# Fifty-six scratch stores of an NSA + RWKV-7 hybrid block move from SyncE's queue to ScalarE's

## The chip, the cores and the metric

One core of one Trainium2 chip. The metric is the device time in microseconds (us) of one execution of the whole program; lower is better. TensorE is called PE here, VectorE DVE, ScalarE ACT, GpSimd POOL, and SyncE, which in this kernel does nothing but issue transfers, SP.

## The reference

One transformer layer on 1024 tokens of width 1024. Two token mixers read the same normed input: native sparse attention (8 query heads, 2 key-value heads; a compressed, a selected and a sliding-window branch, each weighted by a sigmoid gate) and an RWKV-7 recurrence (8 heads of 64). Their outputs are projected, gated by sigmoids, summed, and projected back; a convolutional feed-forward network of width 2816 follows.

```python
h = _rms_norm(x, norm_mix[l])
u = h @ w_in[l]
q, kc, vc, ks, vs, kw, vw, nsa_gl, rw, merge = _split(u, IN_SPLITS)
o_nsa = _nsa(q, kc, vc, ks, vs, kw, vw, nsa_gl, qk_gain[l], cmp_pe[l], cmp_w1[l], cmp_w2[l])
o_rwkv, v_first = _rwkv7(rw, v_first, vres, rwkv_mu[l], ...)
gates = jax.nn.sigmoid(merge.astype(jnp.float32)).astype(x.dtype).reshape(B, S, 2, D)
y = gates[:, :, 0] * (o_nsa @ proj_nsa[l]) + gates[:, :, 1] * (o_rwkv @ proj_rwkv[l])
x = x + y @ w_out[l]
x = x + _conv_ffn(_rms_norm(x, norm_ffn[l]), ffn_up[l], ffn_conv[l], ffn_down[l])
```

With 16 blocks of 64 keys and a top-k of 16 every causal block is selected, so the selected branch is causal attention over all keys.

## The kernel before

Everything is kept transposed: features on the 128 partitions, tokens along the free axis, in two halves of 512 tokens (`H[0]`, `H[1]`; the index `h` in the code). Matrices are split into a 16-bit high and low part, so that one product is three matmuls of 128x512 (`mm3`, line 279, or `mm3s`, line 299, for several products side by side). `wload` loads a 128x1024 weight tile (`wraw`), ACT makes the high part `whi` (line 267), DVE the low part `wlo` (line 269).

The stages, in the order of time:

- Norm of the input and the first projections; then `attention()` (from about 150 to 610 us). For each of four head pairs it takes maxima of scores (`mp`, lines 602 to 609), then makes exp tiles `ph` and `pf` on ACT (lines 672, 673), `pl` on DVE (674), and multiplies with the values (677 to 682). At the end of a pair, four transposes per half go through ACT into `oT`, a tile with one buffer, and from there to scratch memory `onsa_d` (lines 701 to 704).
- Woven between the pieces of attention are "fillers": projections of the RWKV input (`zproj`), of the merge gates (`mproj`: a tanh on ACT into a `zs` buffer, stored to `sg_d`, lines 727 and 728), the low-rank products (`loraproj`, stored to `lw_d`, `al_d`, `gt_d`, line 1055) and the RWKV preludes (`prelude`, which among others copies 32x32 diagonal blocks into `ad` on ACT and stores them to `ad_d`, lines 983 to 985). `zs` has three buffers (`NZS`).
- The RWKV recurrence, eight units of 128 tokens (`front`, `back`; about 610 to 930 us): a chain of short steps on all engines. A unit ends with a group norm (lines 1382 to 1388: a square on ACT, sums on DVE, Ln and Exp on ACT into `gs`, the scaled `yc` on DVE) and four transposes of `yc` on PE. Its output is written to `orw_d` (line 1398). Beside it runs the dense work (`dense`): the rest of `mproj`, then `nsaprep` (reloads `onsa_d` into `hhi`, `hlo`), `nproj`, `oprep` (reloads `orw_d` of the first half into `ohi`, `olo`), `rproj`, `wout0`, and `norm0` (lines 850 to 873: two matmuls with ones, Ln and Exp into `rs`, then the normed tiles `h2h` and `h2l`), and the first feed-forward products `ffn0`.
- From about 940 us the second half: its RWKV output is reloaded (`stg`, `oh`, `ol`), gated and projected, and then the feed-forward network (lines 1669 to 1935) to the end.

What sets the order on each engine is a scheduler in the framework: the code gives every instruction a priority (attention first, fillers 10000 behind it, the recurrence ahead of the dense work), and the scheduler lays the instructions out on a modelled time line and emits one fixed list per engine. Each engine then works through its list in order. A transfer is an instruction in the list of the engine that issues it. It takes the next of eight completion semaphores, which SP and ACT share, and waits first for the transfer that had it before (`DMAHW0` to `DMAHW7` in the lists). In the kernel before, all transfers are issued by SP.

Of the kernel before, what the change touches and what calls it, by code (L numbers as in the profile page):

```python
# [168 lines left out]
def build(tc, D, dbg=None, upto=99):  # L169
    nc = tc.nc  # L170
    V, A, G, T = nc.vector, nc.scalar, nc.gpsimd, nc.tensor
    dbg = dbg or {}

    def load(t, src):
        return nc.sync.dma_start(t, src)

    with ExitStack() as ctx:
# [36 lines left out]
        def ps(tag):  # L214
            b = banks[tag]
            b.append(b.pop(0))
            return pall[:, 512 * b[-1]:512 * b[-1] + 512]
# [14 lines left out]
        H = [slice(0, 512), slice(512, 1024)]  # L232
# [85 lines left out]
        onsa_d = dr.tile([4, 128, S], F32, name="onsa_d")  # L318
        orw_d = [dr.tile([4, 128, 512], F32, name=f"orw_d{h}") for h in range(2)]
        sg_d = dr.tile([16, 128, S], F32, name="sg_d")  # L320
        z_d = dr.tile([14, 128, S], F32, name="z_d")
        lw_d = dr.tile([4, 128, S], F32, name="lw_d")
        al_d = dr.tile([4, 128, S], F32, name="al_d")
        ar_d = dr.tile([8, 128, 2, 512], F32, name="ar_d")
        bk_d = dr.tile([8, 128, 4, 4, 64], F32, name="bk_d")
        ad_d = dr.tile([128, 8, 256], F32, name="ad_d")
# [7 lines left out]
        gt_d = dr.tile([4, 128, S], F32, name="gt_d")  # L334
# [229 lines left out]
        def attention():  # L564
            AQ["q"] = pool("attq", 1, stack=ast, side="right")
            for i in range(2):
                m = AQ["q"].tile([128, 8, 128], F16, name=f"Mt{i}")
# [6 lines left out]
            for i in range(4):  # L574
# [123 lines left out]
                for h in range(2):  # L698
                    pt = ps(OTAG)
                    for t in range(4):  # L700
                        T.transpose(pt[:, t * 128:t * 128 + 128], onat[:, 4 * h + t], ident)
                    oT = AQ["p"].tile([128, 512], F32, name="oT", bufs=1)
                    A.activation(oT, pt, AF.Copy)
                    nc.sync.dma_start(onsa_d[i][:, H[h]], oT)
                    if "oT" in dbg:
                        nc.sync.dma_start(dbg["oT"][i][:, H[h]], oT)

# [16 lines left out]
        def mproj(m, halves):  # L724
            def ev(h, pj):
                sg = FP["f"].tile([128, 512], F32, name="zs", bufs=NZS)
                tanh[0] = A.activation(sg, pj, AF.Tanh, scale=0.5 * WI).ins
                nc.sync.dma_start(sg_d[m][:, H[h]], sg)

            yield from passes(WT[22 + m], hhi, hlo, 8, ev, halves)  # L730

# [181 lines left out]
        def c64(t):  # L913
            return t.rearrange("p (c s) -> p c s", s=64)
# [7 lines left out]
        def prelude(j, h):  # L922
            def tl(name):
                return prep.tile([128, 512], F32, name=name, bufs=1)

            def units(d):
                return d[4 * h:4 * h + 4]

            zk, lw, zr, al, km = (tl(n_) for n_ in ("zk", "lw", "zr", "al", "km"))
            for t, src in ((zk, z_d[4 + j]), (lw, lw_d[j]), (zr, z_d[j]), (al, al_d[j]), (km, km_d[j])):  # L930
                load(t, src[:, H[h]])
            kk, t1, cum, e2 = (tl(n_) for n_ in ("kk", "t1", "cum", "e2"))
            G.tensor_scalar(kk, zk, P("k_k", j), 0.0, op0=ALU.mult, op1=ALU.add)
            A.activation(t1, kk, AF.Square)
            V.tensor_tensor_scan(cum, rmask.rearrange("p c s -> p (c s)"), lw, 0.0, op0=ALU.mult, op1=ALU.add)
            c3 = c64(cum)
            rho = prep.tile([128, 8], F32, name="rho", bufs=1)
            V.tensor_scalar(rho, c3[:, :, 63], 0.5, None, op0=ALU.mult)
            sc = sc_all[:, 4 * h:4 * h + 4, :, j]
            V.tensor_add(sc[:, :, 1], rho[:, 0:8:2], rho[:, 1:8:2])  # L940
            V.tensor_copy(sc[:, :, 0:3:2], rho.rearrange("p (n o) -> p n o", o=2))
            A.activation(sc, sc, AF.Exp)
            E("c3").tensor_tensor(c3, c3, rho[:, :, None].to_broadcast([128, 8, 64]), op=ALU.subtract)
            E("e1").tensor_sub(lw, cum, lw)
            A.activation(lw, lw, AF.Exp)
            A.activation(e2, cum, AF.Exp)
            A.activation(cum, cum, AF.Exp, scale=-1.0)
            E("ar").tensor_mul(e2, zr, e2)
            js = slice(128 * j, 128 * j + 128)
            nc.sync.dma_start(units(ar_d)[:, :, 1, js].rearrange("n p s -> p n s"), j4(e2))  # L950
            E("kh").tensor_mul(km, km, zk)
            E("t1").tensor_mul(zr, zr, km)
            nc.sync.dma_start(rk_d[j][:, H[h]], zr)
            BK = prep.tile([128, 4, 4, 64], F32, name="BK", bufs=1)
            E("b1").tensor_tensor(BK[:, :, 1:3, :], c2(km), c2(cum), op=ALU.mult)
            yield
            logexp()
            pk = ps("P")
            T.matmul(pk, blk, t1, start=True, stop=True)
            V.tensor_scalar(t1, pk, 1e-24, None, op0=ALU.max)  # L960
            A.activation(t1, t1, AF.Ln, scale=float(2.0 ** 30))
            A.activation(t1, t1, AF.Exp, scale=-0.5, bias=kb_)
            E("kk").tensor_mul(kk, kk, t1)
            V.scalar_tensor_tensor(lw, kk, -1.0, lw, op0=ALU.mult, op1=ALU.mult)
            nc.sync.dma_start(units(ar_d)[:, :, 0, js].rearrange("n p s -> p n s"), j4(lw))
            E("ka").tensor_mul(al, kk, al)
            E("b0").tensor_tensor(BK[:, :, 0:4:3, :], c2(al), c2(cum), op=ALU.mult)
            nc.sync.dma_start(units(bk_d)[:, :, j].rearrange("n p q s -> p n q s"), BK)
            yield
            pn = [ps("P"), ps("P")]  # L970
            for n in range(4):
                for o in range(2):
                    for hd in range(2):
                        hr = slice(64 * hd, 64 * hd + 64)
                        c_ = (2 * n + o) * 64
                        T.matmul(pn[hd][64 * o:64 * o + 64, n * 64:n * 64 + 64], BK[hr, n, 3 * o, :],
                                 lw[hr, c_:c_ + 64], start=True, stop=True)
            ad = prep.tile([128, 4, 2, 32], F32, name="ad", bufs=1)
            for o in range(2):
                for b in range(2):  # L980
                    r_ = slice(64 * o + 32 * b, 64 * o + 32 * b + 32)
                    for hd in range(2):
                        A.activation(ad[r_, :, hd], pn[hd][r_, 0:256].rearrange("p (n t) -> p n t", t=64)[
                            :, :, 32 * b:32 * b + 32], AF.Copy)
            nc.sync.dma_start(ad_d[:, 4 * h:4 * h + 4, 64 * j:64 * j + 64], ad.rearrange("p n h t -> p n (h t)"))

        def loraproj():
            def pt(name, tag, dt=FR):
# [17 lines left out]
            for h in range(2):  # L1006
# [6 lines left out]
                for q in range(3):  # L1013
                    x = xs_[q]
                    t = FP["f"].tile([128, 512], F32, name="lx", tag="fu", bufs=3)
# [15 lines left out]
                for j in range(4):  # L1031
                    jc = slice(j * 128, j * 128 + 128)
                    for q in range(3):
                        pj, x = ps("P"), xs_[q]
                        T.matmul(pj, whi[q][:, jc], x, start=True, stop=False)
                        if q == 2:
                            T.matmul(pj, whi[q][:, jc], xl, start=False, stop=False)
                            T.matmul(pj, wlg[:, jc], x, start=False, stop=True)
                        else:
                            o = slice(64 * q, 64 * q + 64)  # L1040
                            T.matmul(pj, wlo[o, jc], x[o], start=False, stop=True)
                        t = FP["f"].tile([128, 512], F32, name="zs", bufs=NZS)
                        if q == 2:
                            A.activation(t, pj, AF.Copy)
                        else:
                            o_ = 14 + 4 * q + j
                            tanh[0] = A.activation(t, pj, AF.Tanh, scale=0.5, bias=pd[:, o_:o_ + 1]).ins
                            c_ = (CW, 0.5)[q]
                            if q == 1:
                                t2 = FP["f"].tile([128, 512], F32, name="zs", bufs=NZS)  # L1050
                                G.tensor_scalar(t2, t, pd[:, 22 + j:23 + j], pd[:, 26 + j:27 + j], op0=ALU.mult,
                                                op1=ALU.add)
                                nc.sync.dma_start(km_d[j][:, H[h]], t2)
                            G.tensor_scalar(t, t, c_, c_, op0=ALU.mult, op1=ALU.add)
                        nc.sync.dma_start((lw_d, al_d, gt_d)[q][j][:, H[h]], t)
                    if j in LY:
                        yield
            logexp()
# [403 lines left out]
        for k in range(4):  # L1462
            t = stage("stg")
# [174 lines left out]
        for i in range(NE):  # L1638
# [8 lines left out]
            for o in range(2):  # L1647
                n = 2 * i + o + PFD
# [339 lines left out]
```

## Time and profile before

| | |
|---|---|
| median of 3 runs | 1666.93 us (1666.73 to 1668.83) |
| the profiled execution | 1667.38 us; its span, from the first to the last instruction, 1665.6 us |
| PE busy | 1624.5 us, 98% |
| DVE, ACT, POOL busy | 71%, 52%, 26% |
| mean granted PE clock | 0.996 |
| the four kinds of store that move | 32 of `sg_d`, 8 of `onsa_d`, 8 of `gt_d` (256 KB each), 8 of `ad_d` (128 KB) |
| when they are issued | `gt_d` 153 to 234 us, `onsa_d` 262 to 610, `ad_d` 323 to 607, `sg_d` 499 to 774 |

Busy shares count neither the issuing of transfers nor waiting. With PE at 98%, the question is where its idle microseconds lie and what ends each of them; a view of waits gives for an engine and a line the engine and line that came last before it went on, with the total, the number of times and the longest. A view of windows gives the busy time of each engine in a stretch, with the granted PE clock and the share of the transfer engines.

### The profile page before, as it was taken

The page shows a single profiled execution, that of the slowest core. Times are in us where ns is not written, and L with a number is a line of the kernel's source. Part 1 is how long each engine was busy: PE and PEld are TensorE (multiplying, and loading weights), DVE is VectorE, ACT ScalarE, POOL GpSimd, SP SyncE. Part 2 cuts the span into 40 slices and gives each one's busy share as a digit, 9 for nine tenths or more (in the row PEclk, how much of TensorE's full clock was granted, in tenths as well). Part 3 has the DMA queues.
Part 4 walks back from the last instruction along what each step waited for, and adds up shares of the span by engine and source line. Part 5 has one row for each costly group of instructions (what it writes and reads, how often), then busy time and mean ns, then how long its engine had stood idle before and what let it go on. Part 6 is the DMA issues. An engine that isn't in the chain of part 4 may idle for free. (4 is left out here: it accounts for less than half of the span.)

```text
span 1665.6 us, 30238 instructions
## 1 busy us (share of the span) xinstructions
PE 1624.5 (98%) x11856; PEld 854.0 (51%) x11856; DVE 1175.5 (71%) x1950; ACT 873.7 (52%) x1569; POOL 436.8 (26%) x352
## 2 busy tenths in 40 slices
PE   7999999999999999999999999999999999999997
PEld 3455555556555555666665444444444444444443
DVE  7445677778877558865547595599677777685898
ACT  5544676657667654555433453554454445645530
POOL 2101131121122220010013200215333433556756
PEclk9999999999999999999999999999999999999999
DMA  6352343242354465435446763453222223623402
GB/s 212 105 146 90 102 148 120 72 135 65 121 163 136 140 204 174 148 121 159 154 156 200 261 238 126 165 172 119 90 76 89 101 77 114 249 78 104 139 26 101
DMA packets 124687, 224.62 MB, mean 135 GB/s; under 512 B 16384, under 2 KB 45440, under 8 KB 124416
## 3 DMA queue, kind: packets, MB, share of 16 engines
q1 hardware_dynamic: 124544, 222.69, 40.6%
q8 instruction: 93, 1.52, 0.4%
q14 instruction: 50, 0.41, 0.1%
HBM read 153.86 MB, written 63.96 MB: 131 GB/s over the span
## 5 line engine op out<-in xcount | busy, mean ns | idle before, releaser
L279 PEld LDWEIGHTS <-whi 128*128 128x128 f16 x1808 | 173.6, 98 | 205.8 <-issue 11.1
L279 PE MATMUL pall<-hlo,whi 128*128 128x512 f16 x608 | 230.1, 380 | 2.1 <-DVE hlo L254 2.1
L279 PE MATMUL pall<-hhi,whi 128*128 128x512 f16 x608 | 229.6, 380 | 0.7 <-DVE zs L714 0.4
L279 PE MATMUL pall<-hhi,wlo 128*128 128x512 f16 x608 | 153.8, 380 | 0.0
L269 DVE SCALAR_TENSOR_TENSOR wlo<-wraw,whi 128x1024 f16<-128x1024 f32 (+1 forms) x98 | 112.7, 1152 | 57.3 <-ACT whi L267 26.0
L267 ACT ACTIVATE whi<-wraw 128x1024 f16<-128x1024 f32 (+1 forms) x98 | 92.7, 950 | 101.6 <-PE pall L279 51.9
L674 DVE TENSOR_TENSOR pl<-pf,ph 128x512 f16<-128x512 f32 (+3 forms) x208 | 118.0, 577 | 38.4 <-ACT pf L673 37.5
L279 PEld LDWEIGHTS <-wlo 128*128 128x128 f16 x904 | 86.4, 98 | 98.1 <-issue 3.9
L672 ACT ACTIVATE ph<-pall 128x512 f16<-128x512 f32 (+3 forms) x208 | 99.8, 480 | 60.8 <-PE pall L667 30.3
L609 DVE TENSOR_REDUCE mp<-pall 128x1 f32<-128x512 f32 (+2 forms) x192 | 95.8, 515 | 34.5 <-PE pall L607 25.8
L673 ACT ACTIVATE pf<-pall 128x512 f32<-128x512 f32 (+3 forms) x208 | 100.3, 482 | 0.0
L1693 DVE SCALAR_TENSOR_TENSOR U<-pall,par,U 128x1023 f32<-128x1023 f32 x64 | 82.1, 1282 | 11.0 <-ACT U L1691 8.9
L1625 POOL TENSOR_TENSOR s<-wraw 128x512 f32<-128x512 f32 x16 | 28.6, 1788 | 191.6 <-DMA wraw<-f_up 184.0
L696 POOL TENSOR_TENSOR onat<-onat,ot 128x256 f32<-128x256 f32 x32 | 28.6, 896 | 139.0 <-DVE ot L695 107.9
L677 PEld LDWEIGHTS <-ph 128*128 128x128 f16 x592 | 55.8, 96 | 16.0 <-ACT ph L672 2.7
L682 PEld LDWEIGHTS <-pl 128*128 128x128 f16 x592 | 55.6, 98 | 14.4 <-DVE pl L674 5.3
L1396 POOL TENSOR_TENSOR b<-b,bonus 128x512 f32<-128x512 f32 x8 | 10.5, 1316 | 197.9 <-ACT b L1394 195.8
L1669 PEld LDWEIGHTS <-whi 128*128 128x128 f16 x384 | 37.6, 98 | 45.3
L1603 DVE SCALAR_TENSOR_TENSOR wlo<-wraw,whi 128x1024 f16<-128x1024 f32 (+1 forms) x35 | 47.5, 1356 | 17.4 <-PE pall L1669 16.3
L680 PEld LDWEIGHTS <-ph 128*128 128x128 f16 x592 | 55.9, 97 | 6.2 <-issue 1.3
L1803 DVE SCALAR_TENSOR_TENSOR acc<-pall,acc 128x512 f32<-128x512 f32 x80 | 51.5, 678 | 8.7 <-PE pall L1801 8.7
L1602 ACT ACTIVATE s12h<-s 128x1024 f16<-128x1024 f32 x16 | 16.9, 1056 | 68.0 <-POOL s L1626 66.7
(581 smaller groups left out, 4372.1 us busy)
## 6 DMA issues: line engine op xcount, KB each, us to landing
wraw<-f_up SPq DMA_DIRECT2D x56, 512.0 KB, 3.3
wraw<-w_t SPq DMA_DIRECT2D x46, 512.0 KB, 3.8
wraw<-f_dn SPq DMA_DIRECT2D x22, 512.0 KB, 3.3
sg_d<-zs SPq DMA_DIRECT2D x32, 256.0 KB, 2.2
wraw<-w_out SPq DMA_DIRECT2D x16, 512.0 KB, 3.9
th_d<-TH SPq DMA_DIRECT2D x32, 256.0 KB, 2.3
z_d<-zs SPq DMA_DIRECT2D x28, 256.0 KB, 2.9
x<-xT SPq DMA_DIRECT2D x24, 256.0 KB, 5.9
```

The costliest lines, as they stand in the source:

```text
L267: A.activation(hi[:, :nk], raw, AF.Copy, scale=WS)
L269: V.scalar_tensor_tensor(lo[:, :nk], raw, WS, hi[:, :nk], op0=ALU.mult, op1=ALU.subtract)
L279: lastm[0] = T.matmul(ps, a[:, k], ks_(b, k), start=(n == 0), stop=(n == 3 * nk - 1)).ins
L609: V.reduce_max(mp[:, x, br, t:t + 1], pm[:, 0:(b1 - b0) * 128], axis=AX.X)
L672: A.activation(ph[0:nkey, rg], pa[0:nkey, rg], AF.Exp, scale=0.125)
L673: A.activation(pf[0:nkey, rg], pa[0:nkey, rg], AF.Exp, scale=0.125)
L674: V.tensor_sub(pl[0:nkey, rg], pf[0:nkey, rg], ph[0:nkey, rg])
L677: T.matmul(pov[:, t, :], ph[0:nkey, tk], vt[0:nkey, kb, g, 0:65], start=first, stop=False, skip_group_check=True)
L680: T.matmul(pov[:, t, 0:64], ph[0:nkey, tk], vt[0:nkey, kb, g, 65:129], start=False, stop=False, skip_group_check=True)
L682: T.matmul(pov[:, t, :], pl[0:nkey, tk], vt[0:nkey, kb, g, 0:65], start=False, stop=True, skip_group_check=True)
L1693: V.scalar_tensor_tensor(u[:, d:1024], c[:, 0:1024 - d], P("conv", 44 * (2 - d) + ci), u[:, d:1024], op0=ALU.mult, op1=ALU.add)
L1803: tick(V.scalar_tensor_tensor(acc[m, h], pj, WI, acc[m, h], op0=ALU.mult, op1=ALU.add))
```

## The change

Four kinds of store are issued from ACT's queue instead of SP's: those whose source tile is last written by ACT. Nothing else in the code changes: sizes, buffers and priorities stay.

```diff
                     A.activation(oT, pt, AF.Copy)
-                    nc.sync.dma_start(onsa_d[i][:, H[h]], oT)
+                    A.dma_start(onsa_d[i][:, H[h]], oT)
...
                 tanh[0] = A.activation(sg, pj, AF.Tanh, scale=0.5 * WI).ins
-                nc.sync.dma_start(sg_d[m][:, H[h]], sg)
+                A.dma_start(sg_d[m][:, H[h]], sg)
...
-            nc.sync.dma_start(ad_d[:, 4 * h:4 * h + 4, 64 * j:64 * j + 64], ad.rearrange("p n h t -> p n (h t)"))
+            A.dma_start(ad_d[:, 4 * h:4 * h + 4, 64 * j:64 * j + 64], ad.rearrange("p n h t -> p n (h t)"))
...
-                        nc.sync.dma_start((lw_d, al_d, gt_d)[q][j][:, H[h]], t)
+                        (A if q == 2 else nc.sync).dma_start((lw_d, al_d, gt_d)[q][j][:, H[h]], t)
```

56 instructions leave SP's list and enter ACT's. Since ACT's modelled time line is now another, the scheduler also lays out PE, DVE and ACT anew from about 150 us on; from about 1000 us on the lists are the same row for row. Three places show it.

ACT's list at the end of the first head pair in attention, before (`ph` and `pf` are the exp tiles of the next pair; the second `oT` needs the first one's buffer and so its store):

```order
L703 ACTIVATE oT<-pall 128x512 [waits PE_49]
L672 ACTIVATE ph<-pall 128x512 [waits PE_49,Activation_49]
L673 ACTIVATE pf<-pall 128x512 [waits Activation_49]
L703 ACTIVATE oT<-pall 128x512 [waits DMAHW1_49,Activation_49]
L961 ACTIVATE t_3320<-t_3320 128x512 [waits DVE_49]
```

And after, with the two stores in it:

```order
L703 ACTIVATE oT<-pall 128x512 [waits PE_49]
L704 DMA onsa_d<-oT 128x512 [waits DMAHW1_49,Activation_49]
L713 ACTIVATE zs<-pall,pd 128x512 [waits DMAHW0_49,PE_49]
L703 ACTIVATE oT<-pall 128x512 [waits DMAHW1_49]
L704 DMA onsa_d<-oT 128x512 [waits DMAHW3_49,Activation_49]
L672 ACTIVATE ph<-pall 128x512 [waits PE_49]
```

Between the two `oT` stood two exp tiles, now one `zs`; the exp tiles are behind both.

ACT's list at the group norm of the second RWKV unit, before (an `ACT_TABLE_LOAD` changes ACT's function table; `zs` is a tanh of `mproj`):

```order
L1382 ACTIVATE ysq<-yc 128x512 [waits DMAHW3_49,DVE_49,Pool_49]
L243 ACT_TABLE_LOAD
L727 ACT_TABLE_LOAD
L727 ACTIVATE zs<-pall 128x512 [waits PE_49]
L1386 ACT_TABLE_LOAD
L1386 ACTIVATE gs<-gs,epst 128x8 [waits DVE_49]
L1387 ACT_TABLE_LOAD
L1387 ACTIVATE gs<-gs 128x8 [waits Activation_49]
```

After, the second unit has one table load there, and the four stand at the third unit, with a store between the Ln and the Exp:

```order
L1382 ACTIVATE ysq<-yc 128x512 [waits DMAHW7_49,DVE_49,Pool_49]
L243 ACT_TABLE_LOAD
L727 ACT_TABLE_LOAD
L727 ACTIVATE zs<-pall 128x512 [waits PE_49]
L1386 ACT_TABLE_LOAD
L1386 ACTIVATE gs<-gs,epst 128x8 [waits DVE_49]
L728 DMA sg_d<-zs 128x512 [waits DMAHW0_49,Activation_49]
L1387 ACT_TABLE_LOAD
L1387 ACTIVATE gs<-gs 128x8 [waits Activation_49]
```

PE's list holds, between the start of this unit's norm and the transposes of its `yc`, eight pieces of line 1221 where the second unit has one before.

ACT's list at `norm0`, before (`zs` is the last square that `norm0` sums, `rs` its Ln and Exp, `h2h` its results, `yhi` a split of the gated second half):

```order
L841 ACTIVATE zs<-xr_11897 128x512 [waits DVE_49,Pool_49]
L267 ACTIVATE whi<-wraw 128x512 [waits DMAHW2_49,PE_49,Activation_49]
L267 ACTIVATE whi<-wraw 128x512 [waits DMAHW4_49,PE_49,Activation_49]
L1473 ACTIVATE yhi<-yt 128x512 [waits DVE_49]
L854 ACTIVATE rs_11929<-pall,epst 128x512 [waits PE_49]
L855 ACTIVATE rs_11929<-rs_11929 128x512 [waits Activation_49]
L1473 ACTIVATE yhi<-yt 128x512 [waits DVE_49]
L872 ACTIVATE h2h_4_11932<-xr_11786 128x512 [waits DVE_49]
```

And after (`oh` are the first tiles of the reloaded second half):

```order
L1465 ACTIVATE oh<-stg 128x512 [waits DMAHW4_49]
L1465 ACTIVATE oh<-stg 128x512 [waits DMAHW5_49]
L841 ACTIVATE zs<-xr_11897 128x512 [waits DVE_49,Pool_49]
L1465 ACTIVATE oh<-stg 128x512 [waits DMAHW6_49]
L854 ACTIVATE rs_11929<-pall,epst 128x512 [waits PE_49]
L855 ACTIVATE rs_11929<-rs_11929 128x512 [waits Activation_49]
L872 ACTIVATE h2h_4_11932<-xr_11786 128x512 [waits DVE_49]
```

`norm0` now comes before the second half's gated products, not among them: PE's list holds 74 matmuls of line 279 between the last unit's `yc` transposes and `norm0` where it held 178, and between the matmuls of line 851 and the first of `ffn0` it holds 10 where it held 24.

## The prediction

> **What bounds the kernel now.** I read the busy shares first, then windows by stage.
>
> ```profile
> PE 1624.5 (98%) x11856; PEld 854.0 (51%) x11856; DVE 1175.5 (71%) x1950; ACT 873.7 (52%) x1569; POOL 436.8 (26%) x352
> ```
>
> PE is busy for 1624.5 of 1665.6 us. Only its 41 idle microseconds, and any stretch at a lower clock, can be won; new idle time can be added anywhere. The windows (stretch, length, then busy us and count of PE, PEld, DVE, ACT, POOL, granted clock, DMA share, GB/s) show where the idle time lies; their first two cover the stretch that the change re-lays:
>
> ```profile
> 150.00:600.00 450.00, 440.43 (x4118) 253.86 (x4116) 331.41 (x720) 301.50 (x676) 89.13 (x91) 1.00 0.38 121
> 600.00:1000.00 400.00, 389.34 (x3923) 230.84 (x3921) 262.71 (x520) 184.21 (x323) 49.89 (x43) 0.99 0.56 183
> 1000.00:1600.00 600.00, 598.79 (x2769) 271.36 (x2768) 438.40 (x489) 301.60 (x417) 238.79 (x156) 1.00 0.35 118
> ```
>
> PE idles 9.6 us in the first, 10.7 in the second, 1.2 in the third, whose order is unchanged. So at most some 20 us are in play on the good side. PE's waits (line, what came last; total, times, longest) name the pieces:
>
> ```profile
> PE pall L299 <- ACT ohi L783: 2.7, 2, 2.2
> PE pall L1165 <- DVE yc L1388: 2.4, 1, 2.4
> PE pall L1262 <- ACT GRB L1257: 1.8, 1, 1.8
> PE pall L663 <- ACT oT L703: 0.8, 1, 0.8
> ```
>
> None names a store; one, of 0.8 us, hangs on a store indirectly (`oT`). SP's queue does wait for the ACT-made tiles:
>
> ```profile
> SPq L728 <- ACT zs L727: 89.1, 24, 7.5
> SPq L704 <- ACT oT L703: 16.1, 7, 5.4
> SPq L1055 <- ACT zs L1044: 11.2, 5, 7.4
> SPq L985 <- ACT ad L983: 8.5, 7, 2.1
> ```
>
> That is 124.9 us in which later loads stand behind a store that isn't ready. This is what the change takes out of SP, and no PE wait above shows a load it made late, except perhaps `ohi` (step F).
>
> **A, SP without the stores.** Besides those 124.9 us SP loses 56 issues:
>
> ```profile
> L728 SPq DMA_DIRECT2D sg_d<-zs x32: 319/320/497, 498.6 to 773.6; - x32
> L704 SPq DMA_DIRECT2D onsa_d<-oT x8: 319/320/383, 262.2 to 609.9; - x8
> ```
>
> 56 x 0.32 = 17.9 us. PE waits for no transfer in this stretch, so I take 0 apart from F: loads come earlier and land in buffers that then sit full.
>
> **B, ACT with the stores.** The same 17.9 us enter ACT's queue if its issue costs what SP's does; no row here shows ACT issuing. ACT is busy 301.5 of 450 and 184.2 of 400 us, so most of it falls into its idle time. What part PE feels I bound by the nearest case of ACT being held, the second `oT` of a pair, which waits for the store of the first:
>
> ```profile
>   DMA onsa_d<-oT: 3.6, 2
> ```
>
> ACT was held 3.6 us there, PE 0.8: a ratio of 0.22. All 56 at 0.22 give +3.9; none gives 0. The 32 `sg_d` and 8 `gt_d` stores follow a filler's tile, with other fillers ready on PE; the 16 others (`onsa_d`, and `ad_d` in attention) stand where ACT feeds PE closely. I take 16 x 0.32 x 0.22 = +1.1.
>
> A transfer issued by ACT also waits for the transfer that held its completion semaphore before, eight transfers back over both queues. Mostly that one has long landed (a landing takes 2.6 us, below); step B prices it at 0, and the first rival is that it isn't.
>
> **C, the `oT` pairs.** An `onsa_d` store takes, from issue to landing (minimum, median, maximum; in the second row the median is the last column), and a `zs` tile on ACT (the ns behind the bar):
>
> ```profile
> DMA to landing us min/median/max: 2.0/2.6/5.6
> ...
> onsa_d<-oT SPq DMA_DIRECT2D x8, 256.0 KB, 2.6
> ...
> L713 ACT ACTIVATE zs<-pall,pd 128x512 f32<-128x512 f32 x28 | 19.3, 688 | 11.8 <-PE pall L279 10.4 <-issue 1.3
> ```
>
> With one `zs` of 0.69 us and its issue between two `oT`, the second waits about 2.6 - 0.69 - 0.32 = 1.6 us. The order has that in two pairs, 3.2 us against 3.6 before: 0, ends -0.8 and +0.8.
>
> **D, the group norm with four table loads.** ACT's and PE's timelines (start, duration) at the 2.4 us wait:
>
> ```profile
> 731.07 1.28 ACT L243 ACT_TABLE_LOAD   x1
> 732.36 1.28 ACT L727 ACT_TABLE_LOAD   x1
> 733.65 0.60 ACT L727 ACTIVATE zs<-pall 128x512 f32<-128x512 f32 x1
> 734.27 1.28 ACT L1386 ACT_TABLE_LOAD   x1
> ...
> 738.16 0.66 PE L1165 MATMUL pall<-cst_f,yc 128*128 128x128 f32 x4 [2.44 <-DVE yc L1388]
> 738.75 1.28 PE L1221 MATMUL pall<-AR,BK 64*128 64x128 f32 x14
> ```
>
> After it the granted clock falls; after the 1.8 us wait that ends at 787.7 it does not, and after the 2.2 us wait of `ohi` it does:
>
> ```profile
> 738.00:745.00 7.00, 6.84 (x75) 4.12 (x76) 1.92 (x7) 3.48 (x8) 2.53 (x2) 0.76 0.14 45
> 787.70:790.00 2.30, 1.63 (x42) 1.43 (x44) 1.21 (x4) 0.92 (x2) 0.00 (x0) 1.00 0.97 224
> 882.60:887.00 4.40, 4.32 (x31) 1.85 (x31) 3.37 (x8) 1.23 (x2) 0.00 (x0) 0.61 0.43 131
> ```
>
> A spell costs 7.0 x 0.24 = 1.7 us at the first, 4.4 x 0.39 = 1.7 at the second. So a gap on PE of somewhere between 1.8 and 2.2 us buys 1.7 us more. In the new order the four loads stand at the third unit, where PE has eight pieces of L1221 ahead of the transposes instead of one: seven more, the 1.28 us of the row of 14. The store between Ln and Exp adds 0.32. Gap 2.44 + 0.32 - 1.28 = 1.48, under 1.8: no spell. D = -0.96 - 1.7 = -2.7; ends -4.1 (gap closed) and +0.3 (the pieces wait too).
>
> [...]
>
> **E, `GRB` at 785 us (1.8 us).** PE's list now has 23 matmuls of L299 ahead of L1262 where it had six: up to 17 x 0.216 = 3.7 us of cover. The pitch is from the chain of waits:
>
> ```profile
> 1160.61 279.02 PE pall L1669 x1292
> ```
>
> 279.02 / 1292 = 0.216. Part of it only moves PE's arrival, so I take -1.0; ends -1.8 and +1.0.
>
> **F, `ohi` (2.2 us and a spell).** On SP the two reloads stand behind stores that wait and other loads; PE comes from the recurrence:
>
> ```profile
> 869.51 3.26 SPq L175 DMA_DIRECT2D y<-np_d  x6
> ...
> 875.72 1.10 SPq L175 DMA_DIRECT2D zs<-orw_d  x2
> ...
> 878.49 0.68 PE L1356 MATMUL pall<-St,QE 64*64 64x64 f32 x16 [0.53 <-DVE St L1347]
> ```
>
> In the new SP list they follow the six `y` loads at once: 872.8 instead of 875.7, 2.9 us earlier. PE's list reaches `ohi` earlier too, by one group each of L1356, L1367 and L1372, three times about 0.63 us = 1.9. Gap 2.2 - 2.9 + 1.9 = 1.2: -1.0, and the spell is saved if the gap stays under about 2, which I count half: -0.85. F = -1.9; ends -3.9 and +2.0.
>
> **G, `norm0`.** It moves ahead of the second half's products:
>
> ```profile
> 975.56 1.02 PE L851 MATMUL pall<-zs,ones 128*128 128x512 f32 x2
> ...
> 976.62 0.69 ACT L854 ACTIVATE rs<-pall,epst 128x512 f32<-128x512 f32 x1 [0.51 <-PE pall L851]
> ...
> 978.95 1.29 ACT L872 ACTIVATE h2h<-xr 128x512 f16<-128x512 f32 x2
> ```
>
> The first `h2h` ends at 979.6, 3.0 us after L851 (976.6). PE had 24 x 0.216 = 5.2 us of products to cover that, and now has ten, 2.2: +0.8. Three prices beside it are guesses of half a 0.63 us ACT row to one row each, for a result that queues behind one more tile: `h2l` 0.3, the square ahead of L851 0.4, the `oh` tiles that now stand around them 0.6. G = +2.1. The first `oh` itself is near its limit: it starts when its reload lands,
>
> ```profile
> 929.28 0.60 PE L1165 MATMUL pall<-cst_f,yc 128*128 128x128 f32 x4
> ...
> 945.70 1.99 ACT L1465 ACTIVATE oh<-stg 128x512 f16<-128x512 f32 x3 [3.40 <-DMA stg<-orw_d]
> ```
>
> and is ready 945.7 + 0.66 - 929.3 = 17.1 us after the `yc` transposes; PE gets there after 74 x 0.216 + 0.6 + 0.86 (transposes, L851) = 17.4. The margin is 0.4. Ends of G: +0.8 (the guesses at nothing) and +6 (`oh` some 4 us late as well, as where one landing of the longest kind, 5.6 us, replaces one of 2.0).
>
> **H, attention.** Its stretches without projections grow (19.4 to 20.1, 13.6 to 15.3, 19.9 to 21.0 us, summed over PE's list at its pitches), 3.5 us in all. In such a stretch PE idles
>
> ```profile
> 370.00:390.00 20.00, 16.72 (x217) 11.29 (x216) 19.14 (x45) 14.25 (x36) 1.27 (x1) 1.00 0.36 107
> ```
>
> 3.3 of 20 us, 0.16; that gives +0.6. The attention total can't grow by it all, since the projections moved out cover idle time elsewhere: +0.3; ends -1 and +4.
>
> **Sum:** 0 + 1.1 + 0 - 2.7 - 1.0 - 1.9 + 2.1 + 0.3 = -2.1. The profiled execution took 1667.38, 0.45 above the median of 1666.93: 1665.3, and 1664.8 against the median.
>
> **The rivals.** Within 0.2% (3.3 us), about what a measurement of this kernel can tell from no change, counts as same.
>
> R1, slower: ACT's queue is in order, and its stores wait. Where the transfer eight back is a late load, ACT stands, and with it the exp tiles or `whi` that PE needs next. If 12 of the 56 wait for a landing of 2.6 us, PE loses 12 x 2.6 x 0.22 = 6.9, giving 1671.7. From four such stores (2.3) it eats the gain of 2.1; from ten (5.7) the result is over 0.2% slower. For it: each store has such a wait in the list, and SP's loads are what ACT now hangs on. Against it: DMA shares of 0.38 and 0.56 say transfers seldom queue. [...]
>
> R2, slower: `norm0`'s stall opens to its end of +6 and takes a spell of 1.7: -2.1 - 2.1 + 6 + 1.7 = +3.5, 1670.4. For it: the margin of 0.4. Against it: one late reload is needed, and SP is emptier.
>
> R3, faster: the gaps of D, E and F close entirely (-1.4, -0.8, -2.0 more) and SP's earlier loads take G down to its end (-1.3): -2.1 - 5.5 = -7.6, 1659.3. For it: with 124.9 us less waiting every load behind runs earlier.
>
> That the stores don't leave SP, or arrive there again through a wait of SP's, is out: the order shows them on ACT, and SP then waits only for the shared semaphores.
>
> **Chances.** The forecast 0.53, spread over its ends: faster 0.12, same 0.38, slower 0.03. R1 0.17 (slower 0.15, same 0.02), R2 0.12, R3 0.18. Faster 0.30, same 0.40, slower 0.30. The range of 8 in 10 runs from 1659.5, about R3's value, to 1674.5, R1 with 16 stores (16 x 2.6 x 0.22 = 9.2 above 1664.8, 1674.0) rounded up; the forecast's own range is 1661.5 to 1668.5.
>
> **What would show it.** On PE: no wait over 2 us for `yc` L1388 and no clock under 0.9 between 700 and 800 us (D); `GRB` under 1 us (E); `ohi` at about 1.2 us with the clock at 1.00 behind it (F); waits of 1 to 2 us around L851 and for `h2h` (G); 0.2 to 0.5 us more idle time in 150 to 600 us (B, H). On ACT: 56 issues of about 0.32 us, and idle time ahead of them put down to a DMA under 10 us in all; over 15 us would be R1. The prediction fails if the shift of the whole order opens a gap on PE in a place that I did not name.

## The result: slower by 0.94%, and the profile after

The changed kernel takes 1682.2 us in the median (1681.9 to 1684.9), the kernel before 1667.9 in the same runs: a ratio of 1.0094, 95% interval 1.0078 to 1.0111. The forecast was 1664.8 with an upper bound of 1674.5. The profiled execution took 1681.85 us, its span is 1680.1, 14.5 us above that of before.

Busy shares first:

```profile
PE 1631.6 (97%) x11856; PEld 857.7 (51%) x11856; DVE 1166.9 (69%) x1950; ACT 872.9 (52%) x1569; POOL 434.8 (26%) x352
```

PE has the same 11856 matmuls. Its busy time grew by 7.1 us and its idle time by 7.4 us, from 41.1 to 48.5. Half clock explains the smaller part of the busy time: by the trace's record of the granted clock it stood at 0.50 for 13.7 us, against 10.2 before (besides a spell at the very end of each span, which has no matmul in it), some 1.7 us. The rest is probably matmuls that follow each other less closely, since a 128x512 matmul is 0.38 us long in the trace (such as the one of L279 at 979.11 us after the change) and one that nothing follows counts whole, where the pitch is 0.216; this was not traced further. Windows show the stages, cut where the last `oT` is made, where the last unit's `yc` is transposed and where the feed-forward network's L1669 begins. Before:

```profile
150.00:609.30 459.30, 449.50 (x4209) 259.13 (x4207) 334.03 (x727) 305.81 (x688) 95.32 (x102) 1.00 0.39 122
609.30:929.30 320.00, 311.05 (x3515) 194.45 (x3514) 209.40 (x442) 144.56 (x257) 34.15 (x25) 0.98 0.51 166
929.30:1150.60 221.30, 219.83 (x1009) 99.39 (x1008) 158.23 (x215) 107.50 (x160) 40.09 (x25) 1.00 0.53 182
```

After:

```profile
150.00:611.40 461.40, 446.84 (x4180) 256.88 (x4179) 333.61 (x727) 304.39 (x683) 90.25 (x96) 1.00 0.38 120
611.40:954.10 342.70, 330.65 (x3586) 204.70 (x3585) 211.72 (x446) 149.70 (x266) 38.63 (x34) 0.99 0.51 166
954.10:1166.20 212.10, 209.31 (x953) 94.42 (x952) 153.60 (x212) 103.22 (x156) 37.94 (x22) 0.99 0.51 176
```

PE's idle time (length less busy) went from 9.8 to 14.6 us in attention, from 9.0 to 12.1 in the recurrence, from 1.5 to 2.8 in the stretch behind it. The stages' lengths can't be compared by themselves, since dense work moved from the third to the second; for the experiments I used a sum that can: of each matmul the distance from its start to the next one's, less the distance that is usual for its kind, added up by stage. By it the changed kernel loses 6.5 us more in attention, 7.5 in the recurrence and 2.9 behind it. These are readings of one trace each: they add up to 16.9 us where the spans differ by 14.5, and a second trace of the changed kernel (`changed_again`, below) gives some 6, 6 and 2.

PE's waits after (those that changed; the last column is the longest):

```profile
PE pall L682 <- DVE pl L674: 4.5, 7, 1.3
PE pall L677 <- ACT ph L672: 2.6, 6, 1.2
PE pall L279 <- ACT oh L1465: 2.2, 1, 2.2
PE pall L299 <- ACT ohi L783: 2.1, 3, 0.9
...
PE pall L299 <- ACT hhi L745: 1.8, 1, 1.8
PE pall L1165 <- DVE yc L1388: 1.6, 1, 1.6
...
PE pall L663 <- ACT oT L703: 1.4, 1, 1.4
...
PE pall L279 <- DVE zs L798: 1.2, 1, 1.2
...
PE pall L279 <- ACT whi L267: 1.1, 1, 1.1
PE pall L279 <- DVE yl L811: 1.0, 1, 1.0
```

`yc` is down to 1.6, as step D had it, and `GRB` is gone, where E had left 0.8. New are `hhi`, `oh`, and three waits for the dense work's own tiles (a fourth, of 0.7 us for `wlo`, stands further down the view). `pl` and `ph` in attention have grown; before they were

```profile
PE pall L682 <- DVE pl L674: 1.8, 4, 1.2
...
PE pall L677 <- ACT ph L672: 1.0, 4, 0.4
```

None of the waits names a store.

The stores themselves, from the answers on their lines after the change:

```profile
L728 ACTq DMA_DIRECT2D sg_d<-zs x32: 326/326/349, 504.8 to 782.4; - x32
...
L704 ACTq DMA_DIRECT2D onsa_d<-oT x8: 326/332/338, 261.4 to 612.0; - x8
```

In the median an issue takes ACT 326 ns for `sg_d` and 332 for `onsa_d`. On ACT's timeline no store of the 56 begins more than 0.4 us after the end of the row ahead of it, and at places it runs beside a row, such as this table load:

```profile
772.51 1.28 ACT L1386 ACT_TABLE_LOAD   x1
772.52 0.33 ACTq L728 DMA_DIRECT2D sg_d<-zs  x1
```

So the first rival, ACT held by its stores' shared semaphores, did not happen in this kernel; its second trace, `changed_again` below, shows no such wait either.

### The profile page after: what moved, and what is told of

Same layout as the page of the kernel before. It is cut to its first block, busy times and chain, and to the rows that moved or that the text cites. A ratio compares the mean times of both kernels' runs of the same rounds, so it can differ in the third digit from the quotient of the medians.

```text
span 1680.1 us, 30189 instructions
## 1 busy us (share of the span) xinstructions
PE 1631.6 (97%) x11856; PEld 857.7 (51%) x11856; DVE 1166.9 (69%) x1950; ACT 872.9 (52%) x1569; POOL 434.8 (26%) x352
## 5 line engine op out<-in xcount | busy, mean ns | idle before, releaser
L279 PEld LDWEIGHTS <-whi 128*128 128x128 f16 x1808 | 174.4, 98 | 213.3 <-issue 16.8
L279 PE MATMUL pall<-hlo,whi 128*128 128x512 f16 x608 | 229.6, 379 | 2.1 <-DVE hlo L254 2.1
L279 PE MATMUL pall<-hhi,whi 128*128 128x512 f16 x608 | 229.1, 379 | 0.6 <-ACT ad L983 0.2
L279 PE MATMUL pall<-hhi,wlo 128*128 128x512 f16 x608 | 153.5, 379 | 0.0
L279 PEld LDWEIGHTS <-wlo 128*128 128x128 f16 x904 | 86.3, 98 | 98.0 <-issue 3.3
L1625 POOL TENSOR_TENSOR s<-wraw 128x512 f32<-128x512 f32 x16 | 32.2, 2010 | 191.0 <-DMA wraw<-f_up 183.4
L1669 PEld LDWEIGHTS <-whi 128*128 128x128 f16 x384 | 37.6, 98 | 45.3
L1603 DVE SCALAR_TENSOR_TENSOR wlo<-wraw,whi 128x1024 f16<-128x1024 f32 (+1 forms) x35 | 47.2, 1349 | 16.6 <-PE pall L1669 12.1
L1602 ACT ACTIVATE s12h<-s 128x1024 f16<-128x1024 f32 x16 | 16.9, 1056 | 68.5 <-POOL s L1626 67.3
```

Of the source, the lines that this page charges most:

```text
L279: lastm[0] = T.matmul(ps, a[:, k], ks_(b, k), start=(n == 0), stop=(n == 3 * nk - 1)).ins
L1669: T.matmul(bank, w[wi][:, o_ + k], xs_[k][xi], start=start and n == 0, stop=n == 11, skip_group_check=True)
```

## The experiments

The change does two things: it moves 56 issues, and it makes the scheduler write another order. To part them, the kernels below (except `only_sg_act`, `all_but_sg_act` and `changed_again`) give every engine a fixed order, and the scheduler may choose only where the moved stores stand. The order is that of another kernel's build, tied row to row by edges that set the order of issue without a wait (the edits below are excerpts; the splices, `after_order_sp_pinned`, `after_order_pl_first` and the kernels with halves carry their finished lists as data):

```diff
-                A.dma_start(sg_d[m][:, H[h]], sg)
+                stq("s").dma_start(sg_d[m][:, H[h]], sg)
...
+        for rows in (order or {}).values():
+            rows = [k for k in rows if k not in skip]
+            for a, b in zip(rows, rows[1:]):
+                tc.add_manual_dep(traced[b], traced[a].name, mybir.DependencyInfo(
+                    mybir.DependencyClass.NoSync, mybir.DependencyReason.DATA), reason="pin")
```

`stq` returns ACT's queue for the kinds of store named by the kernel (`o` for `onsa_d`, `s` for `sg_d`, `a` for `ad_d`, `g` for `gt_d`), else SP's. The traces show that the order held: PE's 11856 matmuls and the rows of DVE and ACT stand as before in `before_order_act_stores`, and as after the change in both kernels that issue that order's stores on SP. Ratios are to the kernel before in the same set of runs, with 95% intervals.

**The queue or the order.** Two theories: the order costs, or the issuing on ACT costs. In the edits `b` is the order of the kernel before, `a` that of the changed kernel, `moved` the 56 stores.

`before_order_act_stores`:

```diff
+    nc, _ = emit(arrays, "osag", b, moved)
```

> Every engine keeps the order of the kernel before; only the 56 stores are issued by ACT, each standing in ACT's list right behind its source tile or a few rows later. Order theory (what costs is the new order of PE, DVE and ACT, not the queue that issues): 1664 to 1670 us, waits on PE as in the kernel before (ohi 2.2, yc 2.4, GRB 1.8), oh not waited for more than 0.5 us. Queue theory (what costs is that ACT issues: 56 x 0.33 us held on an engine that feeds PE, and late tiles behind it): 1676 to 1684 us, with ph, pl and oh waits as in the changed kernel (4.5 us for pl).

Measured: 1668.2 us, ratio 1.0010 (0.9998 to 1.0021), in the order theory's range. `pl` is waited for nearly as before, and `oh` is not among the waits:

```profile
PE pall L682 <- DVE pl L674: 2.1, 4, 1.2
```

`after_order_sp_stores`:

```diff
+    nc, _ = emit(arrays, "", a, moved)
```

> Every engine keeps the order of the changed kernel, but the 56 stores are issued by SP, put into its list where the scheduler finds them ready. Order theory: 1678 to 1684 us, with the waits of the changed kernel: pl 4.5 us in attention, oh about 2 us behind norm0, hhi 1.8 us near 786 us. Queue theory: 1665 to 1671 us.

Measured: 1676.8 us, ratio 1.0057 (1.0038 to 1.0077), and PE's waits are the changed kernel's, although SP issues every store (the trace is of the slowest of six executions, 1681.7 us):

```profile
PE pall L682 <- DVE pl L674: 4.6, 7, 1.4
...
PE pall L677 <- ACT ph L672: 2.5, 5, 1.3
PE pall L279 <- ACT oh L1465: 2.2, 1, 2.2
...
PE pall L299 <- ACT hhi L745: 2.0, 1, 2.0
```

The waits come with the order. The time is a little under the range that I had given for it, which left open whether the queue adds something. So the pair was run again side by side.

> The changed kernel once more, so that it and the next kernel stand beside the same runs of the kernel before: 1680 to 1684 us.

> The order of the changed kernel with the 56 stores on SP, as in after_order_sp_stores, here beside the changed kernel itself. If the order is all: within 2 us of changed_again. If ACT's issuing adds its own cost where cover is thin (the first pair of runs left 0.2 to 0.5% between them): 3 to 8 us below it.

Measured: the changed kernel 1681.9 us, ratio 1.0092 (1.0077 to 1.0107); its order with SP's stores 1680.0, 1.0080 (1.0065 to 1.0096). The order makes 0.57% the first time and 0.80% the second, of 0.92 to 0.94%; the two intervals overlap, so the rest of 0.12 to 0.37% is not settled better than that. The smaller figure is the one from two kernels side by side.

**Which stores.** With the scheduler free:

```diff
+    nc, _ = emit(arrays, "s")        # only_sg_act
+    nc, _ = emit(arrays, "oag")      # all_but_sg_act
```

> Only the 32 sg_d stores go to ACT, the scheduler is free. Its order differs from that of the kernel before in some 2700 PE rows against 13800 from the changed one, so by the order theory it is near before: 1664 to 1672 us. Queue theory, by the share of 32 of 56 stores in a loss of 14.5 us: about 1676 us.

Measured: 1665.3 us, ratio 0.9996 (0.9983 to 1.0009).

> Only onsa_d, gt_d and ad_d, 24 stores, go to ACT, the scheduler is free. Its order is near that of the changed kernel (2200 PE rows differ, against 11000 from before). Order theory: 1676 to 1684 us. Queue theory, 24 of 56 stores: about 1674 us.

Measured: 1673.3 us, ratio 1.0040 (1.0027 to 1.0053), under the order theory's range and at the queue theory's number, which the kernel with `sg_d` alone refutes by 11 us. 32 stores cost nothing that can be seen, 24 others 0.4%, all together 0.94%: that is not a price by store. Each set gives an order of its own.

**Which stage.** The two orders were spliced: one up to a mark, from there the other's order of all that is left; stores on ACT. The lines say how each list was made.

```diff
+    order = spliced(before, last_oT, after)     # att_before_rest_after
+    order = spliced(after, last_oT, before)     # att_after_rest_before
+    order = spliced(before, last_yc, after)     # yc_before_rest_after
+    order = spliced(after, last_yc, before)     # yc_after_rest_before
```

> Every engine keeps the order of the kernel before up to the last oT of attention, and from there on the order of the changed kernel for all that is left; stores on ACT. Stage theory (each stage of the new order costs what its pieces of idle time in the trace of the changed kernel add up to: attention 6.5 us, the recurrence 7.5, the stretch from its last group norm to the feed-forward network 2.9): 1677 us, 1674 to 1680. Attention theory (the attention stage is the cause, what is late later follows from it): 1665 to 1670 us.

Measured: 1675.3 us, ratio 1.0054 (1.0040 to 1.0067).

> The order of the changed kernel up to the last oT of attention, then that of the kernel before for all that is left; stores on ACT. Stage theory: 1673 us, 1671 to 1675. Attention theory: 1676 to 1684 us. If the recurrence and norm0 alone are the cause: 1665 to 1669 us.

Measured: 1674.5 us, ratio 1.0045 (1.0033 to 1.0057).

> The order of the kernel before up to the last unit's group norm, then that of the changed kernel for the rest: norm0 ahead of the second half's products. Stage theory: 1669 us, 1667 to 1671. If norm0's place costs 4 to 8 us by itself: 1670 to 1675 us, with a wait for oh of 2 us or more.

Measured: 1670.9 us, ratio 1.0023 (1.0012 to 1.0035).

The first two fit the stage theory and refute the attention theory. Both have their stores on ACT, which costs 0.10% in the order of before, so of the first mark's 0.45% and 0.54% that much is counted twice: 0.45 + 0.54 - 0.10 = 0.89%, beside the changed kernel's 0.92 to 0.94. Attention's order by itself makes 0.45 - 0.10 = 0.35%, some 5.8 us. The third kernel, with 1670.9 us and the wait for `oh` below, lies in the ranges of both theories that stood for it and doesn't part them. Less the same 0.10%, its 0.23% leaves 0.13%, some 2 us, for the stretch behind the last group norm.

```profile
PE pall L279 <- ACT oh L1465: 2.0, 1, 2.0
```

What is left for the recurrence is 0.54 - 0.23 = 0.31%, some 5 us. By the intervals, each of these differences is good to about 0.2%, 3 us. The fourth splice was to take `norm0`'s place back:

> The order of the changed kernel up to the last unit's group norm, then that of the kernel before for the rest, so that norm0 comes back among the second half's gated products as far as it is still to do; stores on ACT. Stage theory: 1680 us less the 2.9 us of norm0 and oh, 1677 to 1681. If norm0's place costs what I put into the sum's largest rival (oh, a spell, the squares; 4 to 8 us): 1673 to 1677 us.

Measured: 1689.3 us, ratio 1.0133 (1.0115 to 1.0150), outside of what either theory said. In the trace:

```profile
PE pall L279 <- ACT oh L1465: 5.6, 1, 5.6
...
PE pall L279 <- DVE xr L833: 2.6, 1, 2.6
```

A tail of one order behind a head of the other isn't the good tail: `oh` is waited for 5.6 us instead of 2.2. A likely reason, not tested, is that dense work that before's tail counts on as cover is already done in the changed head. For that stretch a stage's cost is thus not a property of its rows alone, and the 2 us above hold behind the head of before.

**An order that nobody meant.** The scheduler, run a second time in one process on the kernel before, gives another order.

```diff
+    a, b = emit(arrays, "osag"), emit(arrays, "")
+    nc = emit(arrays, "", b[1], moved)[0]            # before_other_ties
+    nc = emit(arrays, "osag", b[1], moved)[0]        # other_ties_act_stores
```

> No store moves. The scheduler's second pass over the kernel before, in one process, decides ties in another way: some 860 of 17600 PE rows stand elsewhere, all in the recurrence. If the time follows local luck of the order, this alone moves it by up to 5 us, either way, with the sum of idle time changed between 650 and 930 us only. If only the moved stores matter: 1665 to 1668 us.

Measured: 1661.4 us, ratio 0.9967 (0.9953 to 0.9980). No store moved and the time fell by 5.5 us, a little more than I had allowed. This is a version that beats both kernels. Its PE waits have neither the 2.4 us for `yc` nor the 1.8 for `GRB`, and its ACT list has two table loads fewer: the gain that steps D and E had looked for, from another order. With the stores on ACT in that order:

> The order of before_other_ties with the 56 stores issued by ACT. If the move itself costs what it cost in the order of before (0.1%): 0.9977 of before, 1664 us; if it costs the 0.12 to 0.37% that lie between the two kernels of the changed order: 0.998 to 1.0005; if it gains: under 0.996.

Measured: 1665.3 us, ratio 0.9988 (0.9977 to 1.0000). Here the move alone costs 0.21%, 3.5 us, by the middle values, inside the second of the three cases; the two intervals just touch, and the first case, 0.9977, is not excluded.

**More issues on ACT.** Each of the 56 stores in two halves, in the order of before, once from ACT and once from SP:

```diff
+        n = src.shape[1] // 2
+        self.engine.dma_start(out[:, :n], src[:, :n])
+        self.engine.dma_start(out[:, n:], src[:, n:])
```

> The order of the kernel before, stores on ACT as in before_order_act_stores, each issued as two halves: 112 issues on ACT for 56. If an issue costs PE its 0.33 us x 0.22, as the upper end of step B had it: 4.1 us more than with 56, 1672 us. If ACT's idle time takes it: 1666 to 1669 us.

Measured: 1677.4 us, ratio 1.0062 (1.0047 to 1.0077), more than either case.

> The order of the kernel before, the stores on SP, each issued as two halves (112 issues for 56). If the 0.62% of the halves on ACT is ACT's issuing: 1665 to 1669 us here. If it is the number of transfers and their shared semaphores: 1674 to 1678 us, as on ACT.

Measured: 1668.7 us, ratio 1.0012 (1.0001 to 1.0024). So it is ACT's issuing, with the waits that come with it, and not the number of transfers: 0.50% between the two, 8.3 us for 112 issues. On ACT the second half of a pair takes longer to issue than the first's 326 ns (median 444 for `sg_d`), and once ACT stands for 5 us between two halves; the row behind it gives what ended its idle time, a load of SP's:

```profile
L1987 ACTq DMA_DIRECT2D sg_d<-zs x32: 326/444/947, 503.1 to 784.0; - x32
```

```profile
625.04 0.33 ACTq L1986 DMA_DIRECT2D sg_d<-zs  x1
630.43 0.35 ACTq L1987 DMA_DIRECT2D sg_d<-zs  x1
630.90 1.06 ACT L267 ACTIVATE whi<-wraw 128x1024 f16<-128x1024 f32 x1 [6.98 <-DMA BK<-bk_d]
```

That is what the first rival describes. Of the other kernels with stores on ACT only `only_sg_act` has a store that stands for over 1 us, once, 1.3 us.

**The wait in attention.** DVE's timeline at one of the new `pl` waits, and PE's row:

```profile
251.88 0.68 DVE L674 TENSOR_TENSOR pl<-pf,ph 128x512 f16<-128x512 f32 x1
252.49 1.21 DVE L269 SCALAR_TENSOR_TENSOR wlo<-wraw,whi 128x1024 f16<-128x1024 f32 x1
253.62 0.68 DVE L674 TENSOR_TENSOR pl<-pf,ph 128x512 f16<-128x512 f32 x1
```

```profile
254.36 0.20 PE L682 MATMUL pall<-Vc,pl 128*128 128x65 f16 x1 [1.09 <-DVE pl L674]
```

The second `pl` had its inputs, but a filler's `wlo` of 1.2 us stood ahead of it. In the next kernel, the changed one otherwise, such rows go behind:

```diff
-L269 SCALAR_TENSOR_TENSOR wlo<-wraw,whi 128x1024
-L674 TENSOR_TENSOR pl<-pf,ph 128x512
+L674 TENSOR_TENSOR pl<-pf,ph 128x512 x2
+L269 SCALAR_TENSOR_TENSOR wlo<-wraw,whi 128x1024
```

> The changed kernel, but in DVE's list 16 of the 208 pl tiles of attention move up past the 20 rows of filler work (wlo, BK, zr and the like) that stand between them and their pf. If the attention part of the loss sits in these waits: pl on PE 2 us instead of 4.5, 2 to 4 us less in all, 1678 to 1680 us. If the stretch is short of work on PE anyway: the wait comes back under another name, 1681 to 1683 us.

Measured: 1678.3 us, ratio 1.0067 (1.0053 to 1.0082) against 1.0092 of the changed kernel, and

```profile
PE pall L682 <- DVE pl L674: 2.8, 6, 0.9
```

16 rows on an engine that is busy 69% of the time give back about 0.25%, some 4 us, over half of attention's 0.35 to 0.45%. The two ratios are from different sets of runs and their intervals overlap a little, so the size is loose. The trace, of the slowest of six executions, agrees in the stretch itself: where PE was busy for 446.84 of 461.4 us after the change, it is now

```profile
150.00:611.40 461.40, 449.23 (x4195) 258.12 (x4194) 333.03 (x726) 305.71 (x687) 93.55 (x102) 1.00 0.38 122
```

## Why the prediction was wrong

**Two steps failed: the recurrence (D, E and F) and H.** I had summed -2.1 us; the kernel became 14.3 us slower. By the fixed orders and the splices, attention's order makes some 5.8 us where H had +0.3, the recurrence's some 5 where D, E and F together had -5.6, the stretch behind it some 2 where G had +2.1, and the move itself some 2 where B had +1.1. The larger miss is the recurrence: I priced the new order only at the gaps that the old trace showed and put new gaps at nothing. My last line had named that way of failing.

**Step H.** I priced the new order of attention at +0.3 us by how much longer its stretches without projections had become. The splice gives 0.45%, 7.5 us, and 5.8 without ACT's issuing. Some 0.25% of it, a loose figure, lay not in the length of the stretches but in single places where the order puts a filler's row on DVE ahead of a `pl` that PE is about to need. No experiment moved such rows from ahead of a `ph` on ACT, and the rest stays open. I had the two lists of PE side by side, not those of DVE. Even the upper end that I gave, +4, lies under 5.8, though inside its interval.

**The place I did not name, in the recurrence.** At the end of the recurrence PE waits four times for the dense work's own tiles, 1.2, 1.1, 0.7 and 1.0 us for `zs`, `whi`, `wlo` and `yl`, where before it waited for none. On ACT's and SP's timelines, the one for `whi`:

```profile
918.48 1.06 ACT L267 ACTIVATE whi<-wraw 128x1024 f16<-128x1024 f32 x1 [7.06 <-DMA wraw<-w_out]
```

```profile
910.99 0.46 SPq L175 DMA_DIRECT2D wraw<-w_out  x1
```

The weights are issued at 911.0 and are there at 918.5. The waits for `whi`, `wlo` and `yl` come again in `att_before_rest_after`, whose recurrence has the new order, and not in `att_after_rest_before`, whose recurrence has the old. That the new order has used up the dense work that used to lie here is my reading. No experiment took one of these waits away by itself, so that they make up the recurrence's 5 us is not shown.

**D, E and F were right on the gaps that they named and wrong on the clock.** `yc` waits 1.6 us (I had 1.48), `GRB` no more, `ohi` at most 0.9 (1.2), but 2.1 in all against 2.7 before. But E's gap came back 1.8 us long as `hhi` at 786 us, and the spells that I had subtracted are not saved. Windows of the kernel before (first row) and after:

```profile
797.70:801.10 3.40, 3.40 (x10) 1.19 (x10) 1.35 (x3) 0.30 (x2) 0.00 (x0) 0.50 0.48 160
```

```profile
787.80:798.00 10.20, 10.20 (x81) 7.11 (x78) 5.27 (x12) 7.47 (x13) 0.00 (x0) 0.50 0.56 185
975.50:978.90 3.40, 3.40 (x9) 1.04 (x8) 1.60 (x3) 1.49 (x3) 0.00 (x0) 0.50 1.05 396
```

My rule that a gap of 1.8 us buys no spell fails in the row at 787.80: the wait for `hhi`, 1.8 us, ends at 786.8, and the spell begins at 787.8. The row at 797.70 is a spell that I had not seen; PE was busy for all of the 3.4 us before it, so what it belongs to is open. Without the spell at the very end of each there are 10.2 us at half clock in the old trace, 13.7 in the new one and 10.2 in the second trace of the changed kernel: 0 to +1.7 us where I had put -2.6.

**G had the size, by luck.** I took +2.1, ends +0.8 to +6; the splice gives some 2 us, loose by 3. The parts are others than I had. I had put the first `oh` just in time, with a margin of 0.4 us and 0.6 for its neighbours. PE came to it as I had worked out, 17.4 us behind the `yc` transposes (971.57 less 954.14), but `oh` was not ready at 17.1: ACT waited for its reload, PE could go on only at 19.6, and it stood 2.2 us behind the first matmuls of `norm0`:

```profile
970.55 1.02 PE L850 MATMUL pall<-sq,ones 128*128 128x512 f32 x2
973.77 0.59 PE L279 MATMUL pall<-oh,whi 128*128 128x512 f16 x2 [2.20 <-ACT oh L1465]
974.95 1.57 PE L851 MATMUL pall<-zs,ones 128*128 128x512 f32 x2 [0.58 <-ACT zs L841]
```

A spell followed, the row at 975.50 above. That is the second rival's mechanism at part of its size. In the second trace of the changed kernel `oh` is waited for 1.8 us and no spell follows. The `h2h` that I had priced at 0.8 is not waited for in the first trace and is for 0.7 us in the second.

**B was low, and its ratio is not borne out.** I took +1.1 of 0 to +3.9. With the order held, moving the stores costs 0.10% (-0.02 to 0.21), 0.21% and 0.12 to 0.37%: about 2 to 6 us, and the first of the three is not clear of nothing. The halves give 8.3 / 112 = 0.074 us an issue, close to 0.33 us times the 0.22 that I had from the `oT` row, but that looks like chance: in the same order 56 whole stores cost 1.7 us, 0.03 each, and the 56 issues more add 0.40% beyond what halving costs on SP, 0.12 each. Nor is the ratio fixed: ACT is held for `oT` by its stores for 2.1 us after the change, where PE waits 1.4, and for 7.4 us in `before_order_act_stores`, where PE waits 1.0. What is shown is that issues on ACT can cost and that the price is not the same for each. **A** was right in that no gain from SP's 124.9 us of waiting is to be seen; what there may be is inside the cost of the move. **C**: `oT` is waited for 1.4 us instead of 0.8, inside its ends.

What the runs show of the issue itself: after the change an issue of `sg_d` takes ACT 0.33 us (0.32 on SP before), its landing 2.4 in the median (2.2 before), and no time was gained. With the order held, issuing from ACT, which feeds PE, made the program 0.1 to 0.4% longer.

## What to carry to other kernels

Where a scheduler writes the order, an edit has two effects, its own and that of the order it sets off; hold the order fixed and undo each by itself before giving either a cause. Here a reorder with no edit at all moved the time by -0.33% and the edit's own order by +0.6 to +0.8%, against 0.1 to 0.4% for what the edit does. When reading a new order, look on the engines that feed the bottleneck for long rows of unhurried work that now stand directly ahead of a tile it is about to need; the length of stretches on the bottleneck's own list did not show it. And when a stage is measured in a spliced kernel, subtract what the splice has besides: here the moved stores were in every splice.

## What was not expected of the hardware

Where the granted clock falls to 0.50, it does so in spells whose distances I had not expected. By the trace's record those of the kernel before, the one at the end of the span left out, begin at 739.65, 797.67 and 883.01 us and last 3.413 us each; the beginnings are 58.02 and 85.34 us apart, which is 17.0 and 25.0 times that length. After the change they begin at 787.76 and 975.49 us, 187.73 apart or 55.0 times, and last 10.24 and 3.41 us. That is what two traces show, and not what makes it so. The gaps that I had priced spells by, PE idle for 1.8 to 2.4 us at a time, don't settle where one comes: in the 3.41 us ahead of the spells at 739.65 and 883.01 PE was busy for 1.49 and 1.21, ahead of the one at 797.67 for all of it. Counted in steps of 3.413 us from the start of the span, the spells begin 2.4 us into a step in the trace of before and 2.7 in that of after the change. Executions of one kernel differ too: the eight of `before_other_ties` run from 1658.8 us at a mean clock of 0.999 to 1667.9 at 0.995. A saved spell can't be credited to a gap from one trace.
